# Six stores of normed activations issued by SP in the attention, and the value tiles' transposes in the dense ring

## The chip, the core and the metric

The kernel runs on one core of a Trainium2 chip. The metric is the device time of one execution in microseconds, the median of the runs shown. The core's engines, each with a queue of its own that runs in order, are TensorE (PE in the profile), VectorE (DVE), ScalarE (ACT), GpSimd (POOL) and SyncE (SP, which here only issues DMAs). They wait for one another through semaphores.

## The reference

An encoder of two layers over 1024 prompt rows and 32 sample rows, each row of 1024 numbers in float32. Layer 0 mixes with an mLSTM, layer 1 with a windowed attention of 16 query heads of 64 over 2 shared key and value heads; each layer ends in a SwiGLU FFN. Each sub-layer closes with a layer norm of the weighted residual and its result:

```python
for layer in range(DEPTH):                      # 2
    if layer < N_A_LAYERS:                      # layer 0
        mix, C, n, m = mlstm_mixer(x, ...)
    else:                                       # layer 1
        kv = (x @ w_kv).reshape(B, T, 2, N_KV_HEADS, HEAD_DIM)
        mix = swa(x, k_sh, v_sh, w_q_b[j], sinks_b[j], w_out_b[j], slopes)
    x = layer_norm(DEEPNORM_ALPHA * x + mix, ln_g[layer, 0], ln_b[layer, 0])
    x = layer_norm(DEEPNORM_ALPHA * x + swiglu(x, w_gu[layer], w_down[layer]), ln_g[layer, 1], ln_b[layer, 1])

s = einsum('bcqhgd,bckhd->bchgqk', q, k) * HEAD_DIM ** -0.5 + bias   # own chunk of 64 and the two before it
p = softmax of s with one sink per head
o = einsum('bchgqk,bckhd->bcqhgd', p, v) @ w_out
```

(`swa` stands for the prompt's and the sample's attention, which differ in the cached keys of the sample.) The last 128 prompt rows and the 32 sample rows of K and V are outputs too.

## The kernel before

**Layout.** Activations lie transposed in `ACT`: 128 partitions, 8 k-tiles of 128 features, 1056 columns of rows. The columns are cut in three groups for the products of the attention, `GRP` = (0, 384), (384, 384), (768, 288), and in four quarters of 264 for norms and FFN. A product is three matmuls for each k-tile (`gemm`, L402 to L404): high part by high part, high by low, low by high. The high and low parts of the activations are `sx` (cast on ACT, subtraction on DVE or POOL), of the weights `wh` (cast on ACT, L237) and `wl` (subtraction on POOL or DVE, L239) from the raw load `wr` (SP, L163).

**PSUM.** The products of this stage write to a ring of three banks with the tag `d` ("the dense ring", `psbank`). Another pool, `psb`, has a ring of two with the tag `O`. `v_turn` takes a place there for each transpose of a value tile, and `values` for the outputs of the attention of a head pair and a block.

**The order of the work.** All work is recorded by the program in one order for each engine. A `Weave` runs generators ("tasks") side by side: each product calls `tick` with its estimated microseconds, a task yields the microseconds after which it wants to be called again, and `drain` runs a task to its end. Hence the numbers in `yield` decide where in the engines' queues an instruction stands. They are not waits on the chip.

**The end of layer 0.** `ln_task` with `li == 1` norms one quarter of the columns, in pairs of k-tiles, `kk` = 0 to 3: a multiplication on DVE (L497), scale and shift (ACT L505 or DVE L503), the cast to `sx` on ACT (L511), a store of the pair to `scr` in DRAM (ACT issues it, L513, 264 KB), and the low part (L517, DVE or POOL). There are 16 such stores. What they write is read back as the residual of layer 1 by `mixed_parts`, after 1340 us. The pair `kk` = 3 holds k-tiles 6 and 7, and k-tile 7 is written over by the values (`vT = act[7]`).

**The attention's start.** When quarters 0 and 1 are through, `keys_values(0)` and four `q_group(j, 0)` run while quarters 2 and 3 are still normed: a product in the dense ring, `qh` (ACT, L1657) and `ql` (DVE, L1658), and the task `place`, whose four DMAs on SP (L1664, L1665) put the halves in `Q`. The buffers of `qh` and `ql` are two deep. Then come the transposes of group 0 (`v_turn(0, 0)`, L1736), whose result `v_parts` splits into `VR` (ACT L1678, DVE L1679), the task `attention` (scores on PE, L1763; softmax; `turn`, L1807 to L1811; `values`, L1822; `place`, L1833), and beside it keys and values of groups 1 and 2 with their transposes. The copies of K between partitions (SP, L1623 to L1627) and the stores of the K and V outputs (L1868 to L1871) follow. Last comes a loop over the rest of `QG`, the pairs of a query tile j and a column group g: its first pass makes Q(0,1). `load_bias` (SP, L1689 and L1690) loads the biases of a head pair when the attention begins it.

Of the kernel before, what the change touches and what calls it, by code (L numbers as in the profile page):

```python
# [16 lines left out]
P = 128  # L17
# [48 lines left out]
HALF = T // 2  # L66
# [216 lines left out]
def kernel(ctx: ExitStack, tc: tile.TileContext, A, O):  # L283
    nc = tc.nc
    ctx.enter_context(tc.manual_schedule())
    wv = Weave()
# [3 lines left out]
    def pool(name, space=None, side=None):  # L290
        kw = {}
        if space is not None:
            kw["space"] = space
        if side is not None:
            kw["side"] = side
        return tc.tile_pool(name=name, bufs=1, reuse_waits="tile", **kw)

    def new(p, tag, shape, dt=F32, bufs=1):
        uid[0] += 1
        return p.tile(list(shape), dt, name=f"{tag}_{uid[0]}", tag=tag, bufs=bufs)  # L300
# [72 lines left out]
    ACT = base.tile([P, KT, T], F32, name="act")  # L373
# [8 lines left out]
    scr = dram.tile([P, KT, T], F32, name="scrx")  # L382
# [24 lines left out]
    def psbank():  # L407
        return new(psx[1][0], "d", [P, 512], F32, bufs=psx[1][1])
# [30 lines left out]

    QUARTERS = [(group(g), (g % 2, slice(0, N4))) for g in range(4)]  # L440

    squared, added = set(), set()

    def ln_task(z_, lps, grp, li, last, final):
        cols, (c, zs) = grp
        w = cols.stop - cols.start

        rush = final and grp is QUARTERS[2]
        y = RUSH if rush else LN_PACE[li & 1][last]
        acc = z_[:, 0:2, c, zs]  # L450
        sq = [acc] + [z_[:, 2 + 2 * i : 4 + 2 * i, c, zs] for i in range(3)]
        rs, r2 = z_[:, 8, c, zs], z_[:, 9, c, zs]
        n = KT // 2

        def z2(kk):
            return ACT[:, 2 * kk : 2 * kk + 2, cols]

        def s2(i, kk):
            return SX[:, i, 2 * kk : 2 * kk + 2, cols]

        yield y[0]
        pm = new(lps, "ln", [P, 512], bufs=3 if li & 1 else 2)[:, :w]
        nc.tensor.matmul(pm, onesm[:], acc[:, 0, :], start=True, stop=True)
        yield y[1]
        for s in range(n + 2):
            if s < n:

                nc.vector.tensor_sub(z2(s), pm.unsqueeze(1).broadcast_to([P, 2, w]), z2(s))
            if 1 <= s <= n:
                nc.scalar.activation(sq[s - 1], z2(s - 1), AF.Square)  # L470
            if s >= 3:
                (nc.gpsimd if rush or li & 1 and not (last or s & 1) else nc.vector).tensor_add(acc, acc, sq[s - 2])
            yield y[2]
        if not rush:
            nc.vector.tensor_add(acc[:, 0], acc[:, 0], acc[:, 1])
        added.add((li, cols.start // N4))
        yield y[3] + LN_LAG.get((li, cols.start // N4), 0.0)
        pv = new(lps, "ln", [P, 512], bufs=3 if li & 1 else 2)[:, :w]
        for i in range(1 + rush):
            nc.tensor.matmul(pv, onesm[:], acc[:, i, :], start=(i == 0), stop=(i == rush))  # L480
        squared.add((li, cols.start // N4))
        yield y[4]

        if not li & 1:
            nc.scalar.preload_act_table_set("natural_log_exp_and_others")
        nc.scalar.activation(rs, pv, AF.Ln, bias=eps_ln[:])
        nc.scalar.activation(rs, rs, AF.Exp, scale=-0.5)
        nc.scalar.activation(r2, rs, AF.Square, scale=0.5 ** 0.5)
        yield y[5]
        nc.vector.scalar_tensor_tensor(r2, pv, eps_ln[:], r2, op0=ALU.add, op1=ALU.mult)  # L490
        nc.vector.scalar_tensor_tensor(rs, r2, 1.5, rs, op0=ALU.subtract, op1=ALU.mult)
        if (li, cols.start // N4) == (1, 2):
            while (1, 3) not in added:
                yield 0.2
        for s in range(n + 3):
            if s < n:
                nc.vector.tensor_mul(z2(s), z2(s), rs.unsqueeze(1).broadcast_to([P, 2, w]))  # L497
            kk = s - 1
            if 0 <= kk < n:
                for k in (2 * kk, 2 * kk + 1):  # L500
                    z, gk, bk = ACT[:, k, cols], lng[:, li, k : k + 1], lnb[:, li, k : k + 1]
                    if li & 1 and last and k & 1:
                        nc.vector.tensor_scalar(z, z, gk, bk, op0=ALU.mult, op1=ALU.add)  # L503
                    else:
                        nc.scalar.activation(z, z, AF.Identity, scale=gk, bias=bk)  # L505
            kk = s - 2
            if 0 <= kk < n:
                if final:
                    nc.sync.dma_start(O["y"][:, 2 * kk : 2 * kk + 2, cols], z2(kk))
                else:  # L510
                    nc.scalar.copy(s2(0, kk), z2(kk))  # L511
                    if li == 1:
                        nc.scalar.dma_start(scr[:, 2 * kk : 2 * kk + 2, cols], z2(kk))  # L513
            kk = s - 3
            if kk >= 0 and not final:
                eng = nc.gpsimd if kk & li & 1 else nc.vector
                eng.tensor_sub(s2(1, kk), z2(kk), s2(0, kk).bitcast(F32))  # L517
            yield y[6]
# [194 lines left out]
    cols = [pa.tile([P, 3, 96], F32, name=f"cols{g}") for g in range(3)]  # L713
# [936 lines left out]
    def q_group(j, g):  # L1650

        t0, n = GRP[g]
        ps = project(U_QB[g > 0][j], g)
        q = Q[j, g] = new(pb, "Q", [P, 2, 384], F32R, bufs=4)
        h, l = (new(pb, tag, [P, 384], F32R, bufs=2)[:, :n] for tag in ("qh", "ql"))
        sc = -(HD ** -0.5)
        nc.scalar.activation(h, ps, AF.Copy, scale=sc)  # L1657
        nc.vector.scalar_tensor_tensor(l, ps, sc, h.bitcast(F32), op0=ALU.mult, op1=ALU.subtract)  # L1658

        def place():  # L1660
            yield 1.0
            for i in range(2):
                own, other = slice(64 * i, 64 * i + 64), slice(64 - 64 * i, 128 - 64 * i)
                nc.sync.dma_start(q[own, i, :n].bitcast(F32), h[own].bitcast(F32))  # L1664
                nc.sync.dma_start(q[other, i, :n].bitcast(F32), l[own].bitcast(F32))  # L1665

        return wv.launch(place())
# [7 lines left out]
    def v_parts(c, src, L):  # L1675

        src = src.rearrange("p (g d) -> p g d", g=2)
        nc.scalar.copy(VR[:L, c, :, 0, :], src)  # L1678
        nc.vector.tensor_sub(VR[:L, c, :, 1, :], src, VR[:L, c, :, 0, :].bitcast(F32))  # L1679
# [22 lines left out]
    def keys_values(g):  # L1702
        if g == 2:
            k_part(ck[:], SEQ, P)
        for f, w in ((k_group, U_KV[g > 0][0]), (v_group, U_KV[g > 0][1])):
            f(g)
            if g != 1:
                W.done(w)
# [20 lines left out]
    psb = eb.enter_context(pool("psb", PSUM))  # L1729

    def v_turn(group, pause):
        yield pause
        for c, c0, L, g, off in CH:
            if g == group:
                pt = new(psb, "O", [P, 512], bufs=2)
                nc.tensor.transpose(pt[:L, :P], vT[g][:, off : off + L], ident[:])  # L1736
                v_parts(c, pt[:L, :P], L)
                ast["v"] = c + 1
                yield 0.8
# [116 lines left out]
    for t in spread:  # L1856
        wv.drain(t)
    wv.drain(placing)
    wv.launch(v_turn(0, 0))
    task = wv.launch(attention((GAP_A,) * 8))  # L1860
    ast["ready"] = 4
    for g in range(1, 3):
        keys_values(g)
        wv.launch(v_turn(g, 2.5))
# [8 lines left out]
    def q_made():  # L1873
        yield 4.0
        ast["ready"] += 1

    for i, (j, g) in enumerate(QG):
        if i < 4:
            continue

        while ast["scored"] < 3 * (i - 3):
            wv.tick(0.25)
        q_group(j, g)
        wv.launch(q_made())
        if g == 2:
            W.done(U_QB[1][j])
        if (j, g) == (7, 0):
            nparts[0] = 0
            parts = wv.launch(
                mixed_parts(  # L1890
                    scr,
                    lambda g: ast["ready"] > QG.index((7, g)),
                    lambda k, g: ast["placed"] >= 3 * QG.index((k, g)) + 3,
                    (1.6, 1.0, 1.0),
                )
            )
# [145 lines left out]
```

## Time and profile before

| | us |
|---|---|
| median of the runs | 2210.89 |
| runs | 2210.44, 2210.89, 2212.62 |
| the profiled execution | 2213.98 |
| its span in the profile | 2212.2 |

| engine | busy us | share | instructions |
|---|---|---|---|
| PE | 2175.5 | 98% | 17086 |
| PE's weight loads | 2149.4 | 97% | 17086 |
| DVE | 1455.2 | 66% | 2848 |
| ACT | 1007.9 | 46% | 2259 |
| POOL | 989.8 | 45% | 982 |

The profile covers one execution, the profiled one, whose time is a little above its span. In a row of a timeline stand the start, the duration, the engine, the line of the program, the operation, output<-inputs and shapes; in brackets, how long the engine stood idle before it and which instruction's end let it go on. In the busy times by stretch, a clock of 1.00 is TensorE at its full speed. A DMA's line is that of its issue; its time runs from there to its landing. The 16 stores of L513 were issued from 1134.7 to 1197.6 us, the norm of quarters 2 and 3 ends near 1200, and Q(0,1) is made near 1238.

### The profile page before, as it was taken

The page shows a single profiled execution, that of the slowest core. Times are in us where ns is not written, and L with a number is a line of the kernel's source. Part 1 is how long each engine was busy: PE and PEld are TensorE (multiplying, and loading weights), DVE is VectorE, ACT ScalarE, POOL GpSimd, SP SyncE. Part 2 cuts the span into 40 slices and gives each one's busy share as a digit, 9 for nine tenths or more (in the row PEclk, how much of TensorE's full clock was granted, in tenths as well). Part 3 has the DMA queues.
Part 4 walks back from the last instruction along what each step waited for, and adds up shares of the span by engine and source line. Part 5 has one row for each costly group of instructions (what it writes and reads, how often), then busy time and mean ns, then how long its engine had stood idle before and what let it go on. Part 6 is the DMA issues. An engine that isn't in the chain of part 4 may idle for free.

```text
span 2212.2 us, 44257 instructions
## 1 busy us (share of the span) xinstructions
PE 2175.5 (98%) x17086; PEld 2149.4 (97%) x17086; DVE 1455.2 (66%) x2848; ACT 1007.9 (46%) x2259; POOL 989.8 (45%) x982
## 2 busy tenths in 40 slices
PE   9999999999999999999998999999999999999997
PEld 9999999999999999999998999899999999999997
DVE  4465677787656665566667778888666656466657
ACT  4443455464444444321245778756444444432125
POOL 2544210004655555444525776600665555554441
PEclk9999999999999999999999999999999999999999
DMA  5221213212443343797516433511344434397712
GB/s 170 78 62 57 58 40 87 89 39 86 148 156 145 139 147 135 254 329 231 175 57 174 108 100 97 156 63 39 112 161 156 146 127 156 132 344 256 247 56 79
DMA packets 174499, 298.10 MB, mean 135 GB/s; under 512 B 18064, under 2 KB 130760, under 8 KB 174288
## 3 DMA queue, kind: packets, MB, share of 16 engines
q1 hardware_dynamic: 169936, 290.94, 40.0%
q10 hardware_dynamic: 4352, 4.33, 0.6%
q8 instruction: 135, 2.21, 0.4%
q14 instruction: 76, 0.62, 0.1%
HBM read 201.80 MB, written 82.94 MB: 129 GB/s over the span
## 4 chain that ended last, share of the span: by engine, by line
PE 85%; DVE 6%; DMA 3%; ACT 3%; issue 1%; POOL 1%; SPq 0%; ACTq 0%; POOLq 0%; DVEq 0%
PE d L402 10%; PE d L404 10%; PE d L403 10%; PE A L402 9%; PE A L404 9%; PE A L403 9%; PE B L402 7%; PE B L403 7%; PE B L404 7%; DMA sx<-hs_t 1%; PE T L1807 1%; ACT act L505 1%; DMA hs_x<-z 1%; POOL s L1787 1%; PE T L955 1%
## 5 line engine op out<-in xcount | busy, mean ns | idle before, releaser
L239 POOL TENSOR_TENSOR wl_s<-wr,wh_s 128x512 fp32r<-128x512 f32 x224 | 304.1, 1367 | 237.4 <-ACT wh_s L237 168.9
L402 PE MATMUL d<-sx,wh 128*128 128x264 f32 (+2 forms) x1068 | 341.8, 320 | 2.1 <-ACT wh L237 1.8
L239 POOL TENSOR_TENSOR wl_a<-wr,wh_a 128x512 fp32r<-128x512 f32 x112 | 153.5, 1373 | 409.4 <-ACT wh_a L237 288.2
L404 PE MATMUL d<-sx,wl 128*128 128x264 f32 (+2 forms) x1068 | 325.9, 305 | 2.7 <-POOL wl L239 2.7
L403 PE MATMUL d<-sx,wh 128*128 128x264 f32 (+2 forms) x1068 | 325.3, 305 | 0.4 <-DVE sx L433 0.4
L402 PE MATMUL A<-sx,wh_s 128*128 128x264 f32 x896 | 254.7, 284 | 0.0
L403 PE MATMUL A<-sx,wh_s 128*128 128x264 f32 x896 | 254.4, 284 | 0.0
L404 PE MATMUL A<-sx,wl_s 128*128 128x264 f32 x896 | 254.3, 284 | 0.0
L237 ACT CAST wh_s<-wr 128x512 fp32r<-128x512 f32 x224 | 135.7, 618 | 192.6 <-DVE wr L192 102.7
L402 PEld LDWEIGHTS d<-sx,wh 128*128 128x128 f32 x1068 | 202.3, 189 | 5.5 <-ACT wh L237 2.4
L404 PEld LDWEIGHTS d<-sx,wl 128*128 128x128 f32 x1068 | 201.7, 189 | 3.9 <-POOL wl L239 3.6
L403 PEld LDWEIGHTS d<-sx,wh 128*128 128x128 f32 x1068 | 202.6, 190 | 1.5 <-DVE sx L433 0.7
L402 PE MATMUL d<-sx,ex 128*128 128x264 f32 x624 | 180.7, 290 | 0.1
L403 PE MATMUL d<-sx,ex 128*128 128x264 f32 x624 | 177.3, 284 | 0.0
L404 PE MATMUL d<-sx,ex 128*128 128x264 f32 x624 | 177.1, 284 | 0.0
L404 PEld LDWEIGHTS A<-sx,wl_s 128*128 128x128 f32 x896 | 169.0, 189 | 0.0
L402 PEld LDWEIGHTS A<-sx,wh_s 128*128 128x128 f32 x896 | 168.6, 188 | 0.0
L403 PEld LDWEIGHTS A<-sx,wh_s 128*128 128x128 f32 x896 | 168.6, 188 | 0.0
L1323 POOL TENSOR_TENSOR z<-z 128x528 fp32r<-128x528 f32 x76 | 103.2, 1357 | 126.8 <-ACT z L1322 113.3
L239 POOL TENSOR_TENSOR wl<-wr,wh 128x512 fp32r<-128x512 f32 (+2 forms) x81 | 103.9, 1291 | 94.5 <-ACT wh L237 90.7
L1787 POOL TENSOR_SCALAR s<-s,st 128x256 f32<-128x256 f32 (+1 forms) x144 | 122.8, 865 | 46.6 <-DVE st L1785 29.2
L402 PE MATMUL A<-ex,wh_s 128*128 128x264 f32 x448 | 127.5, 285 | 0.0
(352 smaller groups left out, 7247.4 us busy)
## 6 DMA issues: line engine op xcount, KB each, us to landing
wr<-in_gu SPq DMA_DIRECT2D x92, 512.0 KB
hs_x<-z SPq DMA_DIRECT2D x72, 528.0 KB
hs_t<-z SPq DMA_DIRECT2D x64, 528.0 KB
sx<-hs_x SPq DMA_DIRECT2D x112, 264.0 KB
sx<-hs_t SPq DMA_DIRECT2D x64, 264.0 KB
ex<-hs_t SPq DMA_DIRECT2D x64, 264.0 KB
wr<-in_dn SPq DMA_DIRECT2D x32, 512.0 KB
ex<-hs_x SPq DMA_DIRECT2D x32, 264.0 KB
```

The lines of the kernel that those rows point to most:

```text
L237: self.nc.scalar.copy(hi, r)
L239: eng.tensor_sub(lo, r, hi.bitcast(F32))
L402: nc.tensor.matmul(out, ah, bh, start=start and k == 0, stop=False, **kw)
L403: nc.tensor.matmul(out, ah, bl, start=False, stop=False, **kw)
L404: nc.tensor.matmul(out, al, bh, start=False, stop=stop and k == last, **kw)
L505: nc.scalar.activation(z, z, AF.Identity, scale=gk, bias=bk)
L955: nc.tensor.matmul(pc[:, : 2 * (DV + 1)], keys, vt[j][:, c], start=True, stop=True)
L1323: eng.tensor_sub(lo.bitcast(F32R), buf(s), hi)
L1787: nc.gpsimd.tensor_scalar_mul(p[:R, h, lo:256], p[:R, h, lo:256], st[:R, 2, h : h + 1])
L1807: nc.tensor.transpose(pt[:nk, i, h, :R], p[:R, h, c : c + nk], ident[:R, :R])
```

## The change

Two edits. First: of the 16 stores, the six of quarters 2 and 3 with `kk` below 3 are not issued by ACT in the norm. Their places go to a list, and a new task, launched with the attention's start, issues them on SP: the first when 8.0 estimated microseconds have gone by, the next ones at 2.0 each; those left are issued at once at the first pass of the loop over the rest of `QG`. Pair 3 stays on ACT. Second: the nine transposes of the value tiles take a bank of the dense ring, and not a place in the ring `O`, which then is of the outputs alone.

```diff
@@ ln_task
                     if li == 1:
-                        nc.scalar.dma_start(scr[:, 2 * kk : 2 * kk + 2, cols], z2(kk))
+                        if kk < n - 1 and cols.start >= HALF:
+                            stores.append((2 * kk, cols))
+                        else:
+                            nc.scalar.dma_start(scr[:, 2 * kk : 2 * kk + 2, cols], z2(kk))
@@ v_turn
-                pt = new(psb, "O", [P, 512], bufs=2)
+                pt = psbank()
                 nc.tensor.transpose(pt[:L, :P], vT[g][:, off : off + L], ident[:])
@@ behind ast["ready"] = 4
+    def store():
+        yield 8.0
+        for k, cols in stores:
+            nc.sync.dma_start(scr[:, k : k + 2, cols], ACT[:, k : k + 2, cols])
+            yield 2.0
+
+    storing = wv.launch(store())
@@ for i, (j, g) in enumerate(QG)
         if i < 4:
             continue
+        wv.drain(storing)
```

The lines of the program move by 3 behind the first edit (L1736 becomes L1739), and by 11 behind the new task. In the rows below, `DMAHW` with a number is one of eight semaphores that DMAs take in turn; a DMA that shows one waits for the landing of the DMA that had it before.

ACT, from the last pair of quarter 2 into quarter 3, before:

```order
L511 CAST sx<-act 128x2x264
L513 DMA scrx<-act 128x2x264 [waits DMAHW5_49]
L1657 ACTIVATE qh_14161<-d_14093 128x384 [waits PE_49]
L237 CAST wh_1_14169<-wr_13814 128x512 [waits Pool_49]
L505 ACTIVATE act<-act,lnb,lng 128x264 [waits DVE_49] x2
L511 CAST sx<-act 128x2x264 [waits DVE_49,Activation_49]
L513 DMA scrx<-act 128x2x264 [waits DMAHW7_49]
L505 ACTIVATE act<-act,lnb,lng 128x264 [waits DVE_49]
L511 CAST sx<-act 128x2x264 [waits DVE_49,Activation_49]
L513 DMA scrx<-act 128x2x264 [waits DMAHW3_49]
L237 CAST wh_0_14205<-wr_14001 128x512 [waits Pool_49]
```

And after:

```order
L511 CAST sx<-act 128x2x264
L516 DMA scrx<-act 128x2x264 [waits DMAHW2_49]
L1660 ACTIVATE qh_14158<-d_14093 128x384 [waits PE_49]
L237 CAST wh_1_14166<-wr_13814 128x512 [waits Pool_49]
L505 ACTIVATE act<-act,lnb,lng 128x264 [waits DVE_49] x2
L511 CAST sx<-act 128x2x264 [waits DVE_49,Activation_49]
L505 ACTIVATE act<-act,lnb,lng 128x264 [waits DVE_49]
L511 CAST sx<-act 128x2x264 [waits DVE_49,Activation_49]
L237 CAST wh_0_14200<-wr_14001 128x512 [waits DMAHW5_49,Pool_49]
```

The store of the last pair of quarter 2 stays and has another semaphore; the two of quarter 3 behind it are gone, and nothing else changes its place.

SP, from the stores of the K and V outputs to the placement of Q(0,1), before:

```order
L1868 DMA out_p_k<-kout_13947 128x128
L1869 DMA out_s_k<-kout_13947 128x32
L1870 DMA out_p_v<-act 128x128 [waits DVE_49]
L1871 DMA out_s_v<-act 128x32
L1689 DMA bt_14718<-in_bias 128x2x256 [waits DMAHW4_49]
L1690 DMA sb_14719<-in_bias 32x2x160 [waits DMAHW5_49]
L163 DMA wr_14739<-in_wqb 128x1024 [waits DMAHW6_49,Pool_49]
L1664 DMA Q_14842<-qh_14843 64x384 [waits DMAHW7_49,PE_49,Activation_49]
L1665 DMA Q_14842<-ql_14844 64x384 [waits DMAHW0_49,DVE_49]
L1664 DMA Q_14842<-qh_14843 64x384 [waits DMAHW1_49]
L1665 DMA Q_14842<-ql_14844 64x384 [waits DMAHW2_49]
```

And after, from the last output store:

```order
L1882 DMA out_s_v<-act 128x32 [waits DMAHW0_49]
L1869 DMA scrx<-act 128x2x264 [waits DMAHW1_49]
L1869 DMA scrx<-act 128x2x264 [waits DMAHW2_49]
L1869 DMA scrx<-act 128x2x264 [waits DMAHW3_49]
L1692 DMA bt_14718<-in_bias 128x2x256 [waits DMAHW4_49]
L1693 DMA sb_14719<-in_bias 32x2x160 [waits DMAHW5_49]
L163 DMA wr_14739<-in_wqb 128x1024 [waits DMAHW6_49,Pool_49]
L1667 DMA Q_14842<-qh_14843 64x384 [waits DMAHW7_49,PE_49,Activation_49]
L1668 DMA Q_14842<-ql_14844 64x384 [waits DMAHW0_49,DVE_49]
L1667 DMA Q_14842<-qh_14843 64x384 [waits DMAHW1_49]
L1668 DMA Q_14842<-ql_14844 64x384 [waits DMAHW2_49]
```

Three of the six stores stand ahead of the bias load, and the last two placements of Q(0,1) have the semaphores that two of these stores had before them. Of the other three, two stand farther ahead, one on each side of the bias load before this one, and one among the copies of K.

PE, at the sixth transpose and the product behind it, before:

```order
L1736 MATMUL O_14644<-ident,act 128x128 [waits DVE_49]
L402 MATMUL d_14584<-sx,wh_1_14305 128x288
L403 MATMUL d_14584<-sx,wh_1_14305 128x288
L404 MATMUL d_14584<-sx,wl_1_14306 128x288
L1822 MATMUL O_14651<-hi_14571,VR 128x256 [waits DVE_49,Activation_49]
L1823 MATMUL O_14651<-lo_14572,VR 128x256
```

And after:

```order
L1739 MATMUL d_14641<-ident,act 128x128 [waits Activation_49]
L402 MATMUL d_14580<-sx,wh_1_14299 128x288
L403 MATMUL d_14580<-sx,wh_1_14299 128x288
L404 MATMUL d_14580<-sx,wl_1_14300 128x288
L1825 MATMUL O_14648<-hi_14567,VR 128x256
L1826 MATMUL O_14648<-lo_14568,VR 128x256
```

The sequence is the same; the transpose waits for ACT and no longer for DVE, and the product behind it waits for nothing. The third transpose, at the attention's start, waits for DVE in both.

More of the change, by code (lines that the diff above doesn't have):

```diff
@@ L440 @@
     QUARTERS = [(group(g), (g % 2, slice(0, N4))) for g in range(4)]
-    squared, added = set(), set()
+    squared, added, stores = set(), set(), []
     def ln_task(z_, lps, grp, li, last, final):
```

## The prediction

> **What bounds the kernel now.** I read the page's busy times and its chain first, then PE's timeline for its idle time, then the busy time by stretch where that idle time lies, then the timelines of ACT, POOL, DVE and SP there. The page, busy times and chain:
>
> ```profile
> PE 2175.5 (98%) x17086; PEld 2149.4 (97%) x17086; DVE 1455.2 (66%) x2848; ACT 1007.9 (46%) x2259; POOL 989.8 (45%) x982
> PE 85%; DVE 6%; DMA 3%; ACT 3%; issue 1%; POOL 1%; SPq 0%; ACTq 0%; POOLq 0%; DVEq 0%
> ```
>
> TensorE is busy for 98% and is 85% of the chain. Little more than PE's pauses can be won, 36.7 us in the whole span. The stretches around the change, with start:end, length, busy time and count of PE, PEld, DVE, ACT and POOL, then the granted clock, the DMA share and GB/s:
>
> ```profile
> 1189.00:1203.00 14.00, 7.51 (x37) 5.86 (x36) 11.56 (x19) 9.02 (x20) 9.33 (x8) 0.98 0.65 196
> 1203.00:1206.00 3.00, 3.00 (x12) 3.00 (x11) 0.29 (x1) 0.61 (x2) 2.65 (x4) 0.55 1.02 268
> 1206.00:1224.00 18.00, 17.65 (x126) 16.27 (x125) 11.58 (x51) 11.18 (x39) 10.17 (x16) 1.00 0.41 111
> 1224.00:1247.00 23.00, 20.69 (x145) 19.41 (x144) 15.16 (x59) 17.25 (x55) 17.73 (x22) 1.00 0.49 120
> ```
>
> From 1189 to 1203 PE stands still for 6.5 of 14 us; from 1224 to 1247 for 2.3 of 23; between 1203 and 1206 it runs at about half clock. PE's timeline gives the pauses one by one, in brackets at the row's end, with what ended each:
>
> ```profile
> 1191.66 0.44 PE L402 MATMUL d<-sx,wh 128*128 128x384 f32 x1 [1.32 <-ACT wh L237]
> 1193.48 0.44 PE L404 MATMUL d<-sx,wl 128*128 128x384 f32 x1 [1.21 <-POOL wl L239]
> 1195.93 0.45 PE L402 MATMUL d<-sx,wh 128*128 128x384 f32 x1 [0.44 <-ACT wh L237]
> 1197.29 0.44 PE L404 MATMUL d<-sx,wl 128*128 128x384 f32 x1 [0.73 <-POOL wl L239]
> 1202.31 0.48 PE L1736 MATMUL O<-ident,act 128*128 128x128 f32 x1 [2.80 <-DVE VR L1679]
> 1224.92 0.33 PE L1736 MATMUL O<-ident,act 128*128 128x128 f32 x1 [0.48 <-DVE VR L1679]
> 1226.88 0.36 PE L1822 MATMUL O<-hi,VR 128*128 128x256 f32 x1 [1.24 <-DVE act L1833]
> 1238.19 0.39 PE L1822 MATMUL O<-hi,VR 128*128 128x256 f32 x1 [0.23 <-DVE VR L1679]
> 1244.80 0.39 PE L1763 MATMUL psS<-KH,Q 128*128 128x256 f32 x1 [0.19 <-DMA Q<-ql]
> 1245.47 0.36 PE L1763 MATMUL psS<-KH,Q 128*128 128x256 f32 x1 [0.17 <-DMA Q<-ql]
> ```
>
> The first five are the stretch of the stores; the next three are waits for a place in the outputs' ring of two; the last two are scores that wait for the placement of Q(0,1). What is won by 1245 and not lost there carries to the end, since PE is the chain behind it.
>
> **The stores taken off ACT.** ACT's, POOL's and DVE's timelines around 1190 (ACTq is a DMA issued by ACT):
>
> ```profile
> 1188.15 0.62 ACT L511 CAST sx<-act 128x528 fp32r<-128x528 f32 x1
> 1190.19 0.37 ACTq L513 DMA_DIRECT2D scrx<-act  x1
> 1190.61 0.49 ACT L1657 ACTIVATE qh<-d 128x384 fp32r<-128x384 f32 x1 [1.84 <-PE d L404]
> 1190.99 0.61 ACT L237 CAST wh<-wr 128x512 fp32r<-128x512 f32 x1
> 1188.85 1.32 POOL L517 TENSOR_TENSOR sx<-act,sx 128x528 fp32r<-128x528 f32 x1 [0.78 <-ACT sx L511]
> 1191.68 1.74 POOL L239 TENSOR_TENSOR wl<-wr,wh 128x512 fp32r<-128x512 f32 x1 [1.51 <-ACT wh L237]
> 1192.22 1.36 DVE L503 TENSOR_SCALAR act<-act,lng,lnb 128x264 f32<-128x264 f32 x1
> 1194.12 0.41 DVE L503 TENSOR_SCALAR act<-act,lng,lnb 128x264 f32<-128x264 f32 x1
> ```
>
> The cast ends at 1188.77, the store behind it issues only at 1190.19, and qh and wh stand behind the store. That store (quarter 2, the last pair) stays on ACT, but by the order its wait is for another DMA lane, which fewer stores leave free. So qh starts about 1188.8, wh ends about 1189.8, wl starts when POOL is through with sx at 1190.17 and takes 1.74: the matmul of 1193.48 can go at about 1192.0, 1.5 us earlier. From there the casts are paced by the norm of the quarter on DVE and ACT. One step of it, L503, took 1.36 beside POOL and 0.41 without: 0.95 is what this chain gains if wl moves out of its way, and I take 0.8 as the lower bound of the whole stretch.
>
> The stretch ends with the third value transpose at 1202.31. The chain of waits before it, in time:
>
> ```profile
> 1195.00 5.22 DMA Q<-qh
> 1200.33 0.49 ACT qh L1657
> 1201.36 0.56 DVE ql L1658
> 1201.97 0.30 DVE VR L1679
> ```
>
> A placement of 64 rows took 5.22 us to land, qh waited for it because it frees its buffer, and VR, behind ql on DVE, frees the bank. What a store costs the DMA engines is in ACT's queue, the row with packets, MB and share of 16 engines:
>
> ```profile
> q10 hardware_dynamic: 4352, 4.33, 0.6%
> ```
>
> 0.6% of 2212.2 us over 16 stores is 0.83 us each. Three were issued among these placements and are gone from here: 2.5 us, so the placement lands near 1197.7. qh is then bound by ACT's casts ahead of it and starts near 1198.65, ql follows at once (its own placement has landed too), VR at 1199.8, the transpose at 1200.2: 2.1 us earlier. Upper bound 2.5.
>
> What follows the transpose is slow: the row of 1203:1206 lacks 0.45 of the clock over 3 us and the one of 1189:1203 lacks 0.02 over 14, together 1.35 + 0.28 = 1.6 us. PE's pause ahead of it is 2.80. Elsewhere, PE's timeline at a pause, and the stretch behind it in the columns above:
>
> ```profile
> 1417.45 1.09 PE L1807 MATMUL T<-ident,s 128*128 128x128 f32 x4 [1.45 <-DVE lo L1811]
> 1417.40:1420.80 3.40, 3.35 (x16) 3.38 (x17) 2.47 (x7) 1.82 (x6) 3.39 (x4) 0.51 0.48 151
> ```
>
> There a pause of 1.45 is followed by 3.4 us at 0.51. A pause that is 2.1 shorter can escape it or not: from 0 to 1.6, I take 1.1. First sum of the stores: 2.1 + 1.1 = **3.2 earlier**, bounds 0.8 and 4.1.
>
> The Trainium skill, "TensorE: Matmul & The Clock Gate", "Part 1: The HAM clock gate", says the clock halves after at least one idle window of about 3.4 us. The trace disagrees: half clock after 2.80, and after 1.45. By the page neither pause would have cost any clock, and my 1.1 would be 0; I keep the trace's.
>
> **Transposes in the dense ring.** The rows of 1224.92, 1226.88 and 1238.19 wait for a place in the ring of two: 0.48 + 1.24 + 0.23 = **1.95 removed**. By the order the sixth transpose (1224.92) now waits for nothing slower than ACT's read of an earlier bank, and the product behind it for no place. The third transpose waits, as before, for the subtraction of the first one's bank: nothing there. Bound below: the dense ring's own products could wait for a bank that a transpose holds until VR is read, 0.3 each (the VR row); ten products' worth of matmuls lies between, so I take 0.
>
> **What SP pays.** By the order, one store goes behind each of two stretches in which SP idles, one among the copies of K, and three ahead of the bias load at 1237.03. SP's timeline, and the last link of the chain at 1245:
>
> ```profile
> 1225.77 0.34 SPq L163 DMA_DIRECT2D wr<-in_wqb  x1
> 1236.55 0.43 SPq L1871 DMA_DIRECT2D out_s_v<-act  x1
> 1237.03 0.43 SPq L1689 DMA_DIRECT2D bt<-in_bias  x1
> 1238.07 0.37 SPq L163 DMA_DIRECT2D wr<-in_wqb  x1
> 1238.55 0.47 SPq L1664 DMA_DIRECT2D Q<-qh  x1
> 1239.57 0.47 SPq L1665 DMA_DIRECT2D Q<-ql  x1
> 1240.73 0.59 SPq L1665 DMA_DIRECT2D Q<-ql  x1
> 1240.73 4.61 DMA Q<-ql
> ```
>
> SP issues with hardly a gap here. Four stores at 0.45 (the 0.43 rows, and a gap) are 1.8 us; 0.5 is covered by the wait between 1239.02 and 1239.57, where SP waits for ql from DVE. So Q(0,1) is issued 1.3 later against all else, and scores (0,3) wait for its landing without slack: 0.19 and 0.17 already. Cost **1.3**; bounds 0 (if the 1.8 falls into SP's waits) and 1.3 + 2.5 = 3.8 (if the three stores' 0.83 each also stand ahead of the weight load and Q in the DMA engines). I take 1.3, as the engines were busy for only 0.49 there. PE comes 1.95 earlier to those scores, so the 1.95 is lost in that wait, which grows to 0.36 + 1.95 + 1.3 = 3.6 us. After a pause of that size I expect half clock once, another 1.6.
>
> The Trainium skill, "DMA: Bandwidth & Descriptors", "Issuing engines are not separate DMA queues", speaks against the change: transfers of every issuer run on the same 16 engines, and another issuer saves only issue time. By that the stores' 2.5 counts in full at 1238, and the sum would be 2.5 worse than the one below, 2213.1; no row of before shows stores at that place.
>
> Sum: 3.2 + 1.95 − 1.95 − 1.3 − 1.6 = 0.3 earlier. The profiled execution of 2213.98 (span 2212.2), 3.1 above the median, would be 2213.7; on the median of 2210.89 it gives **2210.6**. Its own range: 2213.0 with the stores at 0.8, to 2209.0 without the half clock of 1245.
>
> **Rivals.**
> A, Q doesn't bind. SP's stores fall into its waits (1239.02, and an issue of a K copy that waits for landings), and Q(0,1) comes as early as its products, which also move by 0.48 + 1.24. Then 3.2 + 1.95 = 5.2 are won: 2205.7. For it: SP waits for DVE even in its fullest stretch. Against: 1.8 of issues do not fit into 0.5.
> B, slower: the three stores delay Q(0,1). Place: SP's weight load and Q behind the stores, by issue and in the DMA engines, and the last two placements wait, by the order, for the landing of stores on their lanes. Q later by 3.8, pause 0.36 + 1.95 + 3.8 = 6.1, stores' gain only 0.8 with the half clock of 1203 left: −0.8 − 1.95 + 5.75 + 1.6 = 4.6 slower, 2215.5. It passes 0.2% from a Q that is 3.6 later. For it: placements take 4.6 us to land even now. Against: DMA share 0.49.
> C, the change does not do what it says: the third transpose still waits for VR, whose ql is paced by the norm on DVE, and the sixth by some other bank; Q is in time, as PE is no earlier. 2210.9.
>
> **How the numbers follow.** 0.2% is 4.4 us, about what a measurement of this kernel can tell from no change. Forecast 0.44, A 0.27, B 0.21, C 0.08. A lies over 4.4 faster, B over 4.4 slower, forecast and C between: faster 0.27, same 0.52, slower 0.21. The range goes from A with the stores at their upper bound (4.1 + 1.95, 2204.8) to B at 2215.5, which leaves out half of B and the tail of A.
>
> **What would show it.** Right: qh near 1188.8 and the third transpose near 1200.2; no pause at the sixth transpose and the product behind; on SP three stores ahead of the bias load, and scores (0,3) with a pause near 3.6 ended by a Q placement. Wrong: third transpose within 1 us of before (stores' term); a pause under 1 us at those scores (A); over 5 us (B); PE's clock at 1.00 through 1203 and 1245 (clock terms).

## The result, and the profile after

The changed kernel takes 2217.96 us (median of 8 runs, 2216.31 to 2220.15), the kernel before 2210.76 beside it (8 runs): a ratio of 1.003, interval 1.002 to 1.004. Run again later, it took 2217.36 beside 2212.40: 1.0021 (1.0012 to 1.0030). It is slower by 5 to 7 us, where I had forecast no change. The first profiled execution took 2219.27 (span 2217.5).

After, page, busy times and chain:

```profile
PE 2180.1 (98%) x17086; PEld 2154.1 (97%) x17086; DVE 1452.1 (65%) x2848; ACT 1008.2 (45%) x2259; POOL 991.9 (45%) x982
PE 88%; DVE 5%; ACT 3%; POOL 2%; issue 1%; DMA 1%; SPq 0%; POOLq 0%; ACTq 0%; DVEq 0%
```

The chain is PE's even more than before. After, the busy time by stretch, with the columns of the prediction:

```profile
1189.00:1203.00 14.00, 9.78 (x40) 8.55 (x40) 10.29 (x20) 8.96 (x20) 9.56 (x7) 0.78 0.45 117
1203.00:1206.00 3.00, 3.00 (x19) 2.93 (x17) 0.69 (x4) 0.48 (x1) 2.79 (x5) 0.91 0.79 232
1206.00:1224.00 18.00, 17.64 (x129) 16.36 (x127) 11.38 (x53) 12.20 (x44) 11.25 (x17) 1.00 0.50 147
1224.00:1247.00 23.00, 17.79 (x120) 16.52 (x119) 13.62 (x54) 14.68 (x45) 16.61 (x22) 0.95 0.68 182
1247.00:1260.00 13.00, 12.66 (x85) 12.57 (x85) 8.39 (x33) 7.43 (x23) 6.50 (x8) 0.83 0.34 77
```

PE now stands for 5.2 us of 1224 to 1247 (2.3 before), and runs below its clock behind it. After, PE's timeline at its pauses, and at the third and sixth transposes:

```profile
1191.67 0.44 PE L404 MATMUL d<-sx,wl 128*128 128x384 f32 x1 [0.93 <-POOL wl L239]
1196.03 0.44 PE L402 MATMUL d<-sx,wh 128*128 128x384 f32 x1 [2.33 <-ACT wh L237]
1197.61 0.69 PE L404 MATMUL d<-sx,wl 128*128 128x384 f32 x1 [0.96 <-POOL wl L239]
1201.41 0.41 PE L1739 MATMUL d<-ident,act 128*128 128x128 f32 x1
1222.57 0.27 PE L1739 MATMUL d<-ident,act 128*128 128x128 f32 x1
1224.44 0.39 PE L1766 MATMUL psS<-KH,Q 128*128 128x256 f32 x1 [0.34 <-DVE st L1772]
1226.10 0.41 PE L1810 MATMUL T<-ident,s 128*128 128x128 f32 x2 [0.41 <-DVE lo L1814]
1236.70 0.63 PE L1810 MATMUL T<-ident,s 128*128 128x128 f32 x4 [0.29 <-DVE lo L1814]
1246.23 0.58 PE L1766 MATMUL psS<-KH,Q 128*128 128x256 f32 x1 [4.17 <-DMA Q<-ql]
1247.36 0.55 PE L1766 MATMUL psS<-KH,Q 128*128 128x256 f32 x1 [0.34 <-DMA Q<-ql]
```

The ring's waits are gone, and three smaller ones of the softmax stand in their place. Scores (0,3), those of head pair 0 and block 3, are the first that read Q(0,1); they wait for 4.17 + 0.34 = 4.5 us, ended by its placement. After, SP's timeline ahead of it, and the last link of the chain there:

```profile
1235.25 0.43 SPq L1882 DMA_DIRECT2D out_s_v<-act  x1
1235.73 1.49 SPq L1869 DMA_DIRECT2D scrx<-act  x3
1237.26 0.50 SPq L1692 DMA_DIRECT2D bt<-in_bias  x1
1238.61 0.43 SPq L163 DMA_DIRECT2D wr<-in_wqb  x1
1240.97 0.61 SPq L1668 DMA_DIRECT2D Q<-ql  x1
1240.97 6.26 DMA Q<-ql
```

SP was 1.3 us ahead of the trace of before at the last output store and is 0.24 behind it at the last placement, which then takes 6.26 to land and not 4.61.

Lined up matmul by matmul, the changed kernel's PE is 1.5 us ahead by 1206 and 2.5 ahead by 1244; with a pause of 4.5 and not 0.36 it is 1.6 behind; it is 3.7 behind by 1252 and 5.3 from 1430 on. The two steps that no pause explains, 2.1 and 1.6, are half clock. After, the stretches around 1245 and 1422, with the columns above:

```profile
1241.00:1244.52 3.52, 1.06 (x6) 0.73 (x5) 0.00 (x0) 0.43 (x1) 2.74 (x4) 1.00 1.01 253
1244.52:1251.34 6.82, 4.78 (x18) 4.42 (x19) 1.81 (x9) 1.20 (x4) 1.80 (x2) 0.50 0.77 167
1418.60:1422.00 3.40, 1.96 (x16) 1.69 (x15) 2.99 (x11) 3.18 (x11) 3.40 (x4) 1.00 0.11 42
1422.00:1428.80 6.80, 6.61 (x33) 6.08 (x31) 4.60 (x12) 3.25 (x9) 3.97 (x4) 0.50 0.58 167
```

Each time 6.8 us at half clock, where before had 3.4 at 1417 and none at 1245.

### The profile page after: what moved, and what is told of

The parts are those of the page before. It is cut to its first block, busy times and chain, and to the rows that moved or that the text cites. A ratio compares the mean times of both kernels' runs of the same rounds, so it can differ in the third digit from the quotient of the medians.

```text
span 2217.5 us, 44259 instructions
## 1 busy us (share of the span) xinstructions
PE 2180.1 (98%) x17086; PEld 2154.1 (97%) x17086; DVE 1452.1 (65%) x2848; ACT 1008.2 (45%) x2259; POOL 991.9 (45%) x982
## 4 chain that ended last, share of the span: by engine, by line
PE 88%; DVE 5%; ACT 3%; POOL 2%; issue 1%; DMA 1%; SPq 0%; POOLq 0%; ACTq 0%; DVEq 0%
PE d L402 10%; PE d L404 10%; PE d L403 10%; PE A L402 10%; PE A L404 10%; PE A L403 10%; PE B L402 7%; PE B L403 7%; PE B L404 7%; PE T L1810 1%; POOL wl L239 1%; POOL s L1790 1%; PE T L958 1%; ACT act L505 1%; PE H L954 1%
```

## Experiments

Theory S says that SP's issues ahead of Q(0,1) delay scores (0,3). Its rivals: the dense ring costs (T), or the norm's stretch without its stores does (N). Later, S splits into the issues themselves (S1) and the bytes in the DMA engines (S2). Times are medians of 11 runs, with that of before beside them; a pause is read from one traced execution of each kernel.

**Each part alone.** The first takes `v_turn`'s edit back, the second the stores':

```diff
 e1: -                pt = psbank()
     +                pt = new(psb, "O", [P, 512], bufs=2)
 e2: the kernel before, with
     -                pt = new(psb, "O", [P, 512], bufs=2)
     +                pt = psbank()
```

> The stores moved as in the change, the transposes left in the outputs' ring. If the stores ahead of the bias load are what makes scores (0,3) wait (theory S), the time stays near the changed kernel's: 2215 to 2219, with a pause of 3.5 to 4.5 us at those scores, since PE comes about 1 us later to a placement that is as late as in the changed kernel. If the transposes in the dense ring are the cost (theory T), it falls back to 2211 or below, and the pause to under 1 us. If taking the stores off ACT is the cost (theory N, the norm's stretch), it is also slow, but with no pause over 1 us at scores (0,3).

> The transposes in the dense ring, the stores as before on ACT. Theory S: 2210 to 2211.5; the ring's three pauses go, 1.0 us is gained by 1244, and it is lost again at scores (0,3), whose pause grows from 0.36 to about 1.4, as the placement of Q(0,1) comes no earlier. Theory T: 2214 or more, with new pauses of the dense ring's products. Theory N: as S.

Stores alone: 2214.88 beside 2212.23, ratio 1.0013 (1.0004 to 1.0022), pauses of 3.87 + 0.64 at scores (0,3). Dense ring alone: 2211.58, ratio 0.9995 (0.9986 to 1.0003). T is out, and N explains no pause there. The stores' time is just under the range expected; its interval meets that of the whole change. The two parts alone add up to 2.0 slower (2.65 and -0.65), the change to 5.0 or more. The 3 us between lie within these intervals taken together, and no run shows whether they are real.

**The stores at another place.** The task's spacing is cut, or the last three stores wait for the next Q products (`late` is 3, and one more after the product of each of the passes 5 to 7):

```diff
 e3: -            yield 2.0
     +            yield 0.5
 e4: -        wv.drain(storing)
     +        for n, (k, cols) in enumerate(stores):
     +            while n >= late[0]:
     +                yield 0.25
```

> Both parts, but the stores 0.5 apart and not 2.0 in the estimated time: by the order four of them stand ahead of the bias load at 1217 and two behind it, all in front of the weight load at 1224, none among the copies of K or ahead of Q(0,1). Theory S: the delay of Q(0,1) is gone; the 1.5 of the norm's stretch stays won, the ring's 1.0 is lost in a pause of about 1.4 at scores (0,3), and the half clock there goes too: 2208 to 2210.5. Theories T and N: the time stays near 2218.

> Both parts, but the three stores that the change issues at once ahead of the bias load come one by one behind the next three Q products, so after the placement of Q(0,1). Theory S: pause at scores (0,3) 1 to 2 us, and 2208 to 2212, the upper end if Q(0,2) is delayed in its turn. Theories T and N: near 2218. A time as low as that of the kernel with all stores early says that it is only the place ahead of Q(0,1) that counts.

All six early: 2211.44 beside 2212.23, ratio 0.9999 (0.9990 to 1.0007). Late: 2213.45, 1.0006 (0.9997 to 1.0015). PE's timeline at scores (0,3), early and late, and of the late kernel SP's two rows around the store that still stands among the copies of K:

```profile
1240.43 0.39 PE L1766 MATMUL psS<-KH,Q 128*128 128x256 f32 x1 [0.39 <-DMA Q<-qh]
1241.12 0.36 PE L1766 MATMUL psS<-KH,Q 128*128 128x256 f32 x1 [0.18 <-DMA Q<-ql]
```

```profile
1244.27 0.36 PE L1766 MATMUL psS<-KH,Q 128*128 128x256 f32 x1 [1.83 <-DMA Q<-ql]
1229.71 1.88 SPq L1627 DMA_DIRECT2D KL<-KL  x1
1231.64 0.59 SPq L1873 DMA_DIRECT2D scrx<-act  x1
```

With the same bytes moved by the same engine, the pause is 0.57 with no store among SP's issues from the weight load near 1224 to Q(0,1), 1.83 with one, and 4.5 with four. S holds. N is out with it: the norm is without its six stores in both, and neither is clear of before. Both times are above what was expected (2208 to 2210.5 and 2208 to 2212); the first expectation counted the norm's 1.5 us as won.

**Issue or bytes.** The first lets ACT issue the three drained stores, the second puts three of 8 KB at their place and the full ones late, the third adds three of 8 KB to the kernel before:

```diff
 e7:  +            eng = nc.scalar if drained else nc.sync
 e8:  as e4, and
      +        if i == 4:
      +            for k, cols in stores[3:]:
      +                cut = slice(cols.start, cols.start + 8)
      +                nc.sync.dma_start(scr[:, k : k + 2, cut], ACT[:, k : k + 2, cut])
 e12: the kernel before, with such three stores at i == 4
```

> The changed kernel, the three stores that stand ahead of the bias load issued by ACT at the same place of the program, not by SP. The bytes are the same, SP's queue is 1.5 us shorter. If SP's issue is what delays Q(0,1) (S1), the pause at scores (0,3) shrinks by 1.3 or more, to about 3, and the time falls by 1.5 to 3 us. If the transfers in the DMA engines are (S2), the pause stays at 4 to 5 us, or grows, since ACT then issues 1.1 us later what it does for the softmax.

> As the kernel with the three late stores one by one behind Q products, but at the place ahead of the bias load stand three stores of 8 columns (8 KB instead of 264 KB), which the full ones repeat later. SP's issues at that place are those of the change, the bytes are gone. S1: pause at scores (0,3) near the changed kernel's, 3.5 us or more, and a time of 2215 or more. S2: pause near that of the kernel without the small stores (1.8), at most 0.5 to 1.3 more, and 2212 to 2215.

> The kernel before with one thing added: three stores of 8 columns (8 KB each, of what is stored already) on SP ahead of the bias load in front of Q(0,1), where the change puts three of its stores. S1: SP issues three times 0.45 to 0.5 later what stands behind, so the pause at scores (0,3), 0.0 to 0.4 in the two traces of before, becomes 1.3 to 1.9, and the time 1.3 to 1.9 above before, or up to 3.5 if a half clock follows. S2 (bytes in the DMA engines): within 0.5 of before, with the pause as before.

Issued by ACT: 2213.69 beside 2212.40, ratio 1.0005 (0.9996 to 1.0014). Three small ones: 2217.60, 1.0022 (1.0013 to 1.0031). Three small ones in the kernel before: 2213.10 beside 2212.05, 1.0006 (0.9997 to 1.0015). The rows, one fence for each kernel, of PE, and of the queue that issues the stores:

```profile
1242.96 0.39 PE L1766 MATMUL psS<-KH,Q 128*128 128x256 f32 x1 [0.26 <-DMA Q<-ql]
1227.34 0.99 ACTq L1872 DMA_DIRECT2D scrx<-act  x2
```

```profile
1234.98 1.46 SPq L1899 DMA_DIRECT2D scrx<-act  x3
1244.26 0.38 PE L1766 MATMUL psS<-KH,Q 128*128 128x256 f32 x1 [3.25 <-DMA Q<-ql]
1245.07 0.36 PE L1766 MATMUL psS<-KH,Q 128*128 128x256 f32 x1 [0.30 <-DMA Q<-ql]
```

```profile
1235.96 1.47 SPq L1884 DMA_DIRECT2D scrx<-act  x3
1245.26 0.36 PE L1763 MATMUL psS<-KH,Q 128*128 128x256 f32 x1 [1.85 <-DMA Q<-qh]
```

The small stores' pause is 3.55, against 1.83 without them: 1.72 for three issues that took 1.46. In the kernel before they bring 1.85, where its two traces had 0.36 and none; against the first, the last placement is issued 1.37 later behind the weight load near 1224, and the pause is 1.49 longer. So the issues alone, without the bytes, make most of it, and the kernel with the small stores takes as long as the changed one. The bytes may add the rest: 4.5 in the first trace of the change (4.08 in the second) is 0.5 to 1.0 over the 3.55. This share is not clean, as the small-store kernel itself issues a full store at 1241.63, while the placements are under way. ACT's run agrees, but is no clean test of bytes: ACT came to these stores some 8 us earlier than SP did, and the fall of 3.7 in time is more than the 1.5 to 3 expected. Its pause of 0.26 is too small a figure, since ACT stood idle for 2.10 us at its stores and PE came 1.8 later to these scores (19.63 against 17.80 us behind the weight load); with PE on time it would be near 2.1. The pause of the last run is as expected; its time alone can't be told from before. Nor do pauses and medians match one to one: the small stores cost 4.15 in the median for 1.72 of pause. The traced execution of that kernel is the fastest of its eleven (2214.66), that of the late kernel the slowest (2216.89), so these two traces can't tell what the other 2.4 are.

**The half clock.** 18 matmuls whose result is not used, ahead of scores (0,3), and the change once more:

```diff
 e6: +            if (j, b) == (0, 3):
     +                pd = psbank()
     +                for _ in range(18):
     +                    nc.tensor.matmul(pd[:, :384], sxh[0][0][:, :P], sxh[0][0][:], start=True, stop=True)
```

> The changed kernel once more, for its time beside the next ones and for a second trace. 2216 to 2220. The pause at scores (0,3) is 4 to 5 us again, as it comes of the order on SP. The half clock near 1200, 1245 and 1420 may differ from the first trace: its windows stand 3.41 us apart and don't start with the kernel, so I expect one or two windows at each place, 1.6 us or so for each.

> The changed kernel with 18 matmuls of 384 columns added on PE ahead of scores (0,3), about 3.2 us of work whose result is not used, into a bank of the dense ring. They fit into the pause of 4.2 us. If a pause of that length costs a half clock behind it (theory H), the clock stays at 1.00 from 1240 to 1255 and the kernel is 1.5 to 3 us faster than the changed kernel beside it. If not, the times are alike, or slower by what of the 3.2 does not fit.

Both 2217.36. With the added matmuls, PE's timeline and the stretch behind:

```profile
1244.56 3.31 PE L1768 MATMUL d<-sx 128*128 128x384 f32 x18
1248.25 0.39 PE L1770 MATMUL psS<-KH,Q 128*128 128x256 f32 x1 [0.37 <-DMA Q<-ql]
1240.00:1256.00 16.00, 15.26 (x104) 14.73 (x104) 7.39 (x26) 7.88 (x22) 8.26 (x10) 1.00 0.69 192
```

And of the changed kernel's second trace the same stretch, and its pauses:

```profile
1240.00:1256.00 16.00, 11.92 (x76) 11.32 (x75) 6.87 (x27) 6.83 (x21) 8.03 (x10) 0.89 0.51 137
1244.73 0.39 PE L1766 MATMUL psS<-KH,Q 128*128 128x256 f32 x1 [3.65 <-DMA Q<-ql]
1245.66 0.36 PE L1766 MATMUL psS<-KH,Q 128*128 128x256 f32 x1 [0.43 <-DMA Q<-ql]
```

In the trace the clock stays at 1.00, and between 1244 and 1252 PE loses 3.5 us against the first trace of before, where the change's second trace loses 5.25 and its first 6.2. But the medians are equal (2214.88 to 2220.73 against 2215.61 to 2219.60). The pause does bring the half clock, as far as the traces go: over all 14, it follows at scores (0,3) in the five in which PE was busy for only 0.15 to 0.46 of the 3.41 us before it, and in no other. That its 1.7 us come back in the time is not shown, and why stays open.

**What the stores' part is worth.** The kernel before once more (8 runs), and the stores early with the transposes in the outputs' ring (`yield 0.5`, no `psbank`):

> The kernel before once more, for a second trace of it. The prediction took the pauses of 1191 to 1203 from one execution. If they are the kernel's own (theory P), they come again: 1.32, 1.21, 0.44, 0.73 and 2.80 within 0.3, and the third transpose 12 us behind 1190. If they were of that execution (theory V: its weight load took 6.5 us to land), they look like those of the kernel with the transposes alone changed: 0.96, 2.35, 0.97 and under 1 at the third transpose, though the six stores are ACT's here too.

> The six stores taken off ACT and issued early on SP (0.5 apart, all ahead of the weight load at 1224), the transposes in the outputs' ring: the stores' part of the change without its delay of Q(0,1). By the prediction's term it gains 3.2: 2209 beside a before of 2212.3. By theory V it gains little or nothing: 2211 to 2213, within the interval of before.

Early stores alone: 2212.37 beside 2212.69, ratio 1.0000 (0.9991 to 1.0008). The kernel before again: 2213.07 beside the same, 1.0001 (0.9991 to 1.0011). The kernel before, PE's timeline in its second trace:

```profile
1191.75 0.44 PE L402 MATMUL d<-sx,wh 128*128 128x384 f32 x1 [0.23 <-ACT wh L237]
1193.57 0.45 PE L404 MATMUL d<-sx,wl 128*128 128x384 f32 x1 [1.19 <-POOL wl L239]
1196.85 0.45 PE L402 MATMUL d<-sx,wh 128*128 128x384 f32 x1 [1.27 <-ACT wh L237]
1198.43 0.69 PE L404 MATMUL d<-sx,wl 128*128 128x384 f32 x1 [0.96 <-POOL wl L239]
1202.08 0.27 PE L1736 MATMUL O<-ident,act 128*128 128x128 f32 x1
```

Pauses of 3.65 us and not 6.5, and none at the third transpose, with the same kernel: the 2.80 there was of one execution. Neither theory's list of pauses is met; their sum is nearer to V's (4.3 and up to 1 more) than to P's (6.5).

**A version without the wait.** Stores early, and the four stores of the K and V outputs two passes of the loop later:

```diff
 e11: as e3, and
      -    nc.sync.dma_start(O["p_k"], kout[:, :P])
      ...
      +        if i == 6:
      +            nc.sync.dma_start(O["p_k"], kout[:, :P])
      ...
```

> Both parts with the stores early as in the kernel with all stores early, and the four stores of the K and V outputs, which stand ahead of Q(0,1) on SP, moved behind it (two passes of the loop later). If SP's queue ahead of Q(0,1) sets the wait at scores (0,3) (S1), the rest of that pause (0.57 in the kernel with early stores) goes, and the time is 2210 to 2211.4, the lowest of all. If not, it is as that kernel, 2211.4, or slower by what the four stores then delay.

2210.78 beside 2212.69, the lowest median, ratio 0.9996 (0.9987 to 1.0005), no pause at scores (0,3). It is clear of the changed kernel, not of the one before.

## Why the prediction was wrong

**The stores' gain, 3.2: the step that failed.** It was read from the pauses of one trace. With the stores off ACT and early the times are the same (2212.37 against 2212.69; the interval of some 2 us to either side leaves out 3.2, though not 0.8), and a second trace of before is itself 3.0 us faster in this stretch than the first. The step-by-step shift was right as far as it went: qh starts at 1188.70 and the matmul of 1193.48 goes at 1191.67. But the wait that it took away was for the most part that execution's. The store ahead of qh waits for the landing of a weight load; it was issued 6.48 us behind that load there, and 5.40, 4.84 and 4.13 in three other traces with the six stores on ACT (the second of before, the transposes alone, the three small stores in the kernel before). And I let POOL's subtraction move for nothing. After, ACT's, POOL's and DVE's timelines:

```profile
1188.70 0.48 ACT L1660 ACTIVATE qh<-d 128x384 fp32r<-128x384 f32 x1
1190.16 1.46 POOL L239 TENSOR_TENSOR wl<-wr,wh 128x512 fp32r<-128x512 f32 x1
1190.52 1.66 DVE L497 TENSOR_TENSOR act<-act,z 128x528 f32<-128x528 f32 x1
1193.18 0.41 DVE L503 TENSOR_SCALAR act<-act,lng,lnb 128x264 f32<-128x264 f32 x1
1195.36 0.61 ACT L237 CAST wh<-wr 128x512 fp32r<-128x512 f32 x1
```

Moved 1.5 us forward, wl lies beside L497, which takes 1.66 and not 0.71; L503 takes 0.41 and not 1.36. The norm loses in one step what it gains in the next, the next cast comes at 1195.36, and PE's 1.5 us become a pause of 2.33. Before, ACT's timeline has that cast at the same time:

```profile
1195.27 0.61 ACT L237 CAST wh<-wr 128x512 fp32r<-128x512 f32 x1
```

That this is not the work of the change is shown by the kernel with the transposes alone, whose six stores are ACT's. Its ACT, POOL, DVE and PE:

```profile
1188.56 0.49 ACT L1657 ACTIVATE qh<-d 128x384 fp32r<-128x384 f32 x1 [0.19 <-issue]
1189.73 1.46 POOL L239 TENSOR_TENSOR wl<-wr,wh 128x512 fp32r<-128x512 f32 x1
1190.10 1.66 DVE L497 TENSOR_TENSOR act<-act,z 128x528 f32<-128x528 f32 x1
1195.60 0.44 PE L402 MATMUL d<-sx,wh 128*128 128x384 f32 x1 [2.35 <-ACT wh L237]
```

The steps and the long pause are the same. PE's pauses up to the third transpose sum to 3.65, 4.28 and 3.85 in these three traces with the stores on ACT, and to 4.22 and 4.36 in the two of the change. The lower bound of 0.8 failed with it: the 0.95 of L503 moved, it was not won. The third transpose, at 1201.41, came 0.90 earlier than in the first trace of before, within the 1 us that I had named as the sign against this term.

**The clock term, 1.1.** It assumed that a shorter pause spares the half clock. Here the pauses were shorter than in the first trace of before (4.2 against 6.5), and the half clock was 6.8 us long all the same in the change's first trace and 3.4 in its second, against 3.4 in both traces of before.

**The ring, 1.95.** The three waits went, as said, and nothing of the dense ring waits. But 1.0 is won (1.5 ahead at 1206, 2.5 at 1244), as scores and transposes of the softmax now wait 0.34, 0.41 and 0.29. That it is lost again at scores (0,3) was right.

**What SP pays, 1.3, bounds 0 and 3.8.** The mechanism was the right one, the size was short. Against the first trace of before SP lost 1.75 of issue (1.51 ahead at the weight load of 1224, 0.24 behind at the last placement), and the landing 1.65. I held the DMA engines for half idle, from a mean of 0.49 over 23 us; where the change's placements wait, from 1241 to 1244.5, their share was 1.01. The pause forecast, 3.6, came out at 4.1 to 4.5. Put together from the runs: 0.57 is there with early stores, 1.26 comes from the one store among the copies of K, 1.72 from three issues, and 0.5 to 1.0 is left for their bytes. Each is a difference of single traces, and the two traces of before differ by 0.36 in this pause, those of the change by 0.43, so the last part is hardly more than that.

**The half clock behind it, 1.6.** It came, at 2.1 and 1.5 in the two traces.

With the stores at 0 and SP's part as measured, the sum is 1.0 won, 3.7 to 4.2 lost in the pause beyond the 0.36 of before, and 1.5 to 2.1 in clock: 4.2 to 5.3 slower, which meets the second comparison's 5.0. Of the 5.3 between that and the forecast of 0.3 earlier, 3.2 are the stores' term and 1.4 to 1.9 SP's. The first comparison's 7.2 is 2.2 more, most of it in the kernel before (2210.76 there, 2212.40 in the second); why is not shown. **Rival B** had the place, the sign and nearly the time, with a stores' gain of 0.8 that is not there, and a pause of 6.1 that is 4.5. I gave it 0.21. **A** failed on the first point: SP's stores did not fall into its waits. They can, when moved: in the kernel with all six early they do, and it is no faster than before. **C** was wrong in its means and right in one point: what the norm paces stayed where it was.

The DMA sentence of the Trainium skill ("DMA: Bandwidth & Descriptors", "Issuing engines are not separate DMA queues") calls the issuer's time usually small beside the transfer. One by one that is so here: SP issued a placement in 0.6 us, and it took 4.6 to 6.3 to land. But issues in a row add up ahead of what waits: 1.72 us of pause for three issues of 8 KB, against 0.5 to 1.0 that is left for the bytes of the full stores.

## What to carry to other kernels

Before a queue that issues back to back, count the issues ahead of the transfer that something waits for, whatever their size: a store that nobody waits for belongs behind it, or into a stretch in which the queue idles. Take pauses that hang on landings from two traces before a term of 3 us is built on them, and a transfer engine's share from the 2 or 3 us ahead of the wait, not from the mean of the stage.

## What the hardware showed

The half clock came in pieces of 3.41 us, one or two on end, on a grid that starts elsewhere in each execution; this agrees with the free-running window of 3413 ns in the Trainium skill ("TensorE: Matmul & The Clock Gate", "Part 1: The HAM clock gate"). It does not take an idle window, though: it followed windows in which PE was busy for 0.30 (1241 to 1244.5 above) and 0.58 of the time (1418.6 to 1422), and over all traces for 0.15 to 0.61, while others of 0.49 to 0.66 had none. So the same pauses cost the same kernel a window of some 1.6 us more or less: the ring's waits near 1225 brought none in the first trace of before and one in its second. Of the first trace's 5.3 us against before, 1.6 came at 1422, behind a pause of 1.44 us that both kernels have.
